# Output-weight loads moved from SyncE's DMA queue to ScalarE's in a hybrid Fourier/SSD mixer layer

## The chip, the cores and the metric

The kernel runs on one core of a Trainium2 chip. The metric is the device time of one execution in microseconds; the figure to compare is the median of several runs. TensorE (PE) does the matrix products, VectorE (DVE), ScalarE (ACT) and GpSimd (POOL) the elementwise work, and SyncE (SP) starts the DMA transfers. Loads of TensorE's stationary operand are listed as PEld.

## The reference

One layer of a generator over 2048 latent tokens with 256 context tokens, model width 1024. A modulated RMSNorm feeds one input projection, whose columns split into a Fourier group and an SSD (Mamba-2) group; both are gated, joined and sent through one output projection of 2048 by 1024.

```python
def token_mixer(h, rows, cols, w_in, ...):
    u, zf, zs, xbc, dt_raw = jnp.split(h @ w_in, PROJ_SPLITS, axis=-1)
    four = fourier_mixer(u, zf, w_fourier, b_fourier)
    xbc = depthwise_conv_grid(xbc, conv_w, conv_b, rows, cols)
    ssd, h_f, h_b = ssd_mixer(xbc, dt_raw, zs, ..., h0_f, h0_b)
    return jnp.concatenate([four, ssd], axis=-1), h_f, h_b

def fourier_mixer(u, zf, w_f, b_f):
    uf = u.astype(jnp.float32).reshape(bsz, length, N_FOURIER_GROUPS, FOURIER_GROUP)
    mixed = jnp.fft.fft2(uf, axes=(1, 3), norm='ortho').real.reshape(bsz, length, D_FOURIER)
    mixed = mixed.astype(u.dtype) @ w_f + b_f
    return mixed * jax.nn.silu(zf)

# in reference(), for the one layer:
    hx = rmsnorm(x, norm_w[i]) * (1.0 + scale[:, None]) + shift[:, None]
    x_mix, _, _ = token_mixer(hx, rows, GRID_W, *layer, h_f, h_b)
    x = x + gate[:, None] * (x_mix @ w_out[i])
    return rmsnorm(x, final_norm_w)
```

The products are computed with operands split into a high and a low part (float32r), so that one product of the reference is three matrix products in the kernel: high by high, high by low and low by high.

## The kernel before, in words

The kernel runs in stages that overlap at their ends.

1. Normalisation and transposition give the normalised input as two large tiles, `hh` (high) and `hl` (low), each 128 partitions by 8 by 2048. Then follow the input projections, the convolution and the preparation of the SSD scan. In the convolution stage the output weights are also scaled, split and stored to the DRAM scratch `wo_d` (16 blocks of 128 rows, high and low).
2. A backward scan writes its share of the SSD output to DRAM (`yb_d`).
3. The Fourier stage. `f_table` and `f_step2` prepare the tables `ab` and the intermediate `xf`, which lie in the room of `hh` and `hl` that is no longer needed. `f_mm(dt, h, i)` is half of a product for one of four channel tiles `dt` (in the order 0, 3, 1, 2) and one half `h` of the frequencies: 12 matrix products into one PSUM tile of tag `mm`, of which there are six. After the second half (i = 1) `f_gate` copies it to the tile `q32` on ScalarE (one buffer), VectorE makes the sum and the difference `yy` (two buffers), and GpSimd and VectorE multiply them into the gate table `zf`. `zf` holds the gate of one channel tile, 128 by 2048, has two buffers, and is loaded by `zf_load` from `zfT_d`; the finished product is stored from the same tile to `fm_d`. So the third and the fourth `zf` load wait for the stores of the first and the second tile. The eight products run in the order (0,0), (0,1), (3,0), (3,1), (1,0), (2,0), (1,1), (2,1), as (dt, h).
4. The units. The last stage handles 64 units, one per chunk c of 128 tokens and group g of 6 heads, in steps: `s1` loads decay rows (`rt`, `lt`), `cb` and `chl`, makes the arguments `parg` on TensorE, their exponential `w` on ScalarE and the product `w` times `cb` on VectorE; `s2` loads `yb`, `zs`, `xg` and `bt` and applies the carried state (`pyo`); `s3` advances the state (`pst`); `s4` makes the chunk's output (`py`) and its gate; `s5` normalises it (`pn`, `mh`, `ml`); `s6` does the output projection (`po`) with the weights `wos` and the Fourier part `fm`, which `fm_half` loads from `fm_d`. The loop body for u has s1 and s2 of unit u + 1, s3 and s4 of u, s5 of u - 1, s6 of u - 2.

The output weights come back from `wo_d` in four groups of four blocks, one group for each g; a block is two loads (high and low). `wplace` gives their places, all in the room of `hh` and `hl`:

```python
    wplace = [((hl, 1536), (hh, 1536)), ((hl, 0), (hl, 1024)), ((hl, 512), (hh, 1024)), ((hh, 0), (hh, 512))]
```

Group 0 takes the last quarter of both tiles, free when the last gate projection has read it. Group 1 takes room of `xf` for h = 0, group 2 that for h = 1, and group 3 that of the tables `ab`, which every Fourier product reads.

What sets the order: the instructions are written in Python, and a scheduler lays them out per engine by the order of writing and a model of when each becomes ready; each engine then executes its list in order and waits at an instruction whose inputs or room are not there. `tc.issue_after(ins)` around a block adds that its instructions come behind `ins` on the engine of `ins`. `interleave` mixes the list `side` of Fourier steps with the last projections; what is left of it is issued just before the units. Before the change every DMA is begun by SyncE through `load` (line 63), the weight loads too. Group 0 is issued behind the interleaved part, group 1 as a step of `side` ahead of the last two Fourier products, groups 2 and 3 in the unit loop at u = 0 and 1, behind the last `fm_d` store (`fo["st"]`) and the `bt` load of the next unit. The helper `copy` (line 68) is a ScalarE activation; line 72 is the low part of a split.

Of the kernel before, what the change touches and what calls it, by code (L numbers as in the profile page):

```python
# [9 lines left out]
F32 = mybir.dt.float32  # L10
# [29 lines left out]
def rev(ap):  # L40
    dims = [list(d) for d in ap.ap]
    off = ap.offset
    for d in dims[1:]:
        off += d[0] * (d[1] - 1)
        d[0] = -d[0]
    return bass.AP(ap.tensor, off, dims)
# [3 lines left out]
def mixer_layer(ctx: ExitStack, tc: tile.TileContext, A: dict, out: bass.AP, taps=None):  # L50
    nc = tc.nc
    mm = nc.tensor.matmul

    def pool(name, bufs=1, space=None, stack=ctx, side=None):
        kw = {"space": space} if space is not None else {}
        if side is not None:
            kw["side"] = side
        if space != DRAM:
            kw["reuse_waits"] = "tile"
        return stack.enter_context(tc.tile_pool(name=name, bufs=bufs, **kw))  # L60

    def load(dst, src):
        return nc.sync.dma_start(out=dst, in_=src).ins
# [3 lines left out]
    def copy(dst, src):  # L67
        return nc.scalar.activation(dst, src, AF.Copy).ins  # L68
# [8 lines left out]
    def scratch(name, shape, dtype=F32):  # L77
        return dram.tile(list(shape), dtype, name=name)
# [14 lines left out]
    wo_d = scratch("wo_d", [16, P, 2, D], F32R)  # L93
# [46 lines left out]
    p1 = ctx.enter_context(ExitStack())  # L140
# [70 lines left out]
    with ExitStack() as p0, tc.issue_after(pre):  # L211
# [130 lines left out]
        for op in 'n1 n2 m1 n3 m2 m3'.split():  # L342
            if op == "n1":
                norm_finish(xn1, hh, hl, 512, 0)
            elif op[0] == "n":
                b = int(op[1])
# [3 lines left out]
            else:  # L350
                b = int(op[1])
# [4 lines left out]
    with ExitStack() as pu:  # L356
# [144 lines left out]
        for n2 in range(16):  # L501
# [3 lines left out]
            for k in range(KT):  # L505
                a = hh[:, k].rearrange("p (a b) -> p b a", b=16)[:, n2]
                b = hl[:, k].rearrange("p (a b) -> p b a", b=16)[:, n2]
# [3 lines left out]
            with tc.issue_after(mu):  # L511
                if n2 in dt_work:
                    fn, i = dt_work[n2]
# [257 lines left out]
    with ExitStack() as psc:  # L771
        sp = pool("sp3", 2, stack=psc)
        st = {}
# [60 lines left out]
        side = []  # L834
# [3 lines left out]
        for n, a in enumerate(seq):  # L838
            if n + AHEAD < len(seq):
                side.append((0.0, scan_prep(*seq[n + AHEAD])))  # L840
            dr, c, g = a
# [7 lines left out]
    wos = {}  # L849
# [3 lines left out]
    def w_load(n):  # L853
        r, k = 2 * (n % 4), worder[n]
        wos[k] = tuple(t[:, r:r + 2, c:c + 512] for t, c in wplace[n // 4])
        for i in range(2):
            load(wos[k][i].bitcast(F32), wo_d[k, :, i].rearrange("p (a b) -> p a b", a=2).bitcast(F32))

    def w_group(g):
        for n in range(4 * g, 4 * g + 4):  # L860
            w_load(n)
# [10 lines left out]
    fo = {"new": main_psum}  # L872
# [23 lines left out]
    def zf_load(dt):  # L896
        def go():
            zf = zft[dt] = fb.tile([P, 16, P], F32, name="zf", tag="zf")
            load(zf[:].rearrange("p a b -> p (a b)"), zfT_d[dt])
            if dt != 2:  # L900
                nc.scalar.activation(zf, zf, AF.Silu)
            nc.gpsimd.tensor_tensor(out=zf[:, :, 64], in0=zf[:, :, 64], in1=ye[:, dt], op=ALU.mult)
        return go

    def f_table(j):
        def go():
            for i in range(2):
                pa = main_psum()
                mm(pa, c64[i], wfs[j], start=True, stop=True)
                copy(ab(i, 0, j), pa)  # L910
                nc.vector.tensor_tensor(out=ab(i, 1, j), in0=pa, in1=ab(i, 0, j).bitcast(F32), op=ALU.subtract)
            if j < 3:
                g_load(0, j + 1)
        return go
# [30 lines left out]
    def f_gate(dt, p0, p1, parts):  # L945
        zf = zft[dt]
        q32 = fb.tile([P, 512], F32, name="q32", tag="q32", bufs=1)
        copy(q32, p1)
        for sign in range(2):
            yy = fb.tile([P, 512], F32, name="yy", tag="yy")  # L950
            nc.vector.scalar_tensor_tensor(out=yy, in0=p0, scalar=bf[:, dt:dt + 1], in1=q32,
                                           op0=ALU.add, op1=ALU.add if sign == 0 else ALU.subtract)
            for yv, k1, nt in parts[sign](yy):
                a = k1 if sign == 0 else P - k1 - nt * yv.shape[-1] + 1
                zv = zf[:, :, a:a + nt * yv.shape[-1]]
                if sign == 1:
                    zv = rev(zv)
                if nt > 1:
                    zv = zv.rearrange("p a (t b) -> p t a b", t=nt)
                (nc.vector if sign else nc.gpsimd).tensor_tensor(out=zv, in0=yv, in1=zv, op=ALU.mult)  # L960

    def f_mm(dt, h, i):
        def go():
            po = fo[i] = fo["new"]()
            f_half(po, dt, i, lambda *a: xf(*a, h))
            if i == 0:
                return

            def cut(yy):
                return yy[:].rearrange("p (t a b) -> p t a b", t=8, b=4)  # L970

            def minus(yy):
                if h:
                    return [(cut(yy), 32, 8)]
                return [(cut(yy)[:, 0, :, 1:4], 1, 1), (cut(yy)[:, 1:], 4, 7)]

            f_gate(dt, fo[0], fo[1], (lambda yy: [(cut(yy), 32 * h, 8)], minus))
            if h == 1:
                fo["st"] = store(fm_d[:, :, dt, :].rearrange("c p w -> p c w"), zft[dt])
        return go  # L980
# [28 lines left out]
    side = [(1.7, f_table(j)) for j in range(4)]  # L1009
# [8 lines left out]
    for n, (dt, h) in enumerate(fmm):  # L1018
        if n in (4, 5):
            side.append((0.0, zf_load(dt)))  # L1020
        if n == 6:
            side.append((0.0, lambda: w_group(1)))
        side += [(2.6, f_mm(dt, h, i)) for i in range(2)]
    left = interleave(zs_ops([(i, (3,)) for i in range(19, 7, -1)]), side, 10, .75)
    wa1 = P2["wa1"]
# [16 lines left out]
    w_group(0)  # L1042
    for _, fn in left:
        fn()
    p1.close()
    ps = pool("ps2", space=PSUM)
    fo["new"] = lambda: ps.tile([P, 512], F32, name="pft", tag="out", bufs=2)
    pre2 = preload(LNEXP)
    units = {}

    def s1(u):
        c, g = divmod(u, G)
        d = units[u] = {}
        if g == 0:
            sml = wa1.tile([P, 3, H], F32, name="sml4", tag="sml")
            load(sml, smf_d[:, c])
        else:
            sml = units[u - 1]["sml"]
        d["sml"] = sml
        r, l = rt[u % 2], lt[u % 2]  # L1060
        cs = slice(c * P, c * P + P)
        for dr in range(2):
            hsl = slice(dr * H + g * HG, dr * H + (g + 1) * HG)
            load(r[32 * dr + 12:32 * dr + 14, :].rearrange("o (h w) -> o h w", w=P).bitcast(F32),
                 cum_d[:, hsl, cs].bitcast(F32))
            for s in range(2):
                load(l[32 * dr + 6 * s:32 * dr + 6 * s + 6, dr].bitcast(F32), q_d[s, hsl, cs].bitcast(F32))
        cb = wa1.tile([P, P], F32, name="cb", tag="cb")
        load(cb, cb_d[c, :, g])
        chl = wa1.tile([P, 2, P], F32R, name="chl", tag="chl")  # L1070
        load(chl[:].bitcast(F32), chl_d[c, :, g].bitcast(F32))
        d["chl"] = chl
        w = wa1.tile([P, HG, P], F32, name="w", tag="w")
        for h2 in range(2):
            cols = slice(384 * h2, 384 * h2 + 384)
            pa = []
            for dr in range(2):
                po = ps.tile([P, 3, P], F32, name="parg", tag="arg", bufs=2)
                mm(po, l[:, dr], r[:, cols], start=True, stop=True)  # L1079
                pa.append(po)  # L1080
            nc.vector.copy_predicated(out=pa[0], mask=msk[:].unsqueeze(1).broadcast_to([P, 3, P]), data=pa[1])  # L1081
            with tc.issue_after(pre2):
                d["exp"] = nc.scalar.activation(w[:, 3 * h2:3 * h2 + 3], pa[0], AF.Exp).ins  # L1083
        nc.vector.tensor_tensor(out=w, in0=w, in1=cb[:].unsqueeze(1).broadcast_to([P, HG, P]), op=ALU.mult)  # L1084
        d["w"] = w
# [162 lines left out]
    for u in range(NU + 2):  # L1248
        if u + 1 < NU:
            if u > 0:  # L1250
                s1(u + 1)
            s2(u + 1)
        if u < 2:
            with tc.issue_after(fo["st"]), tc.issue_after(units[u + 1]["ld"]):
                w_group(u + 2)
        if u < NU:
            s3(u)
            s4(u)
        if 1 <= u <= NU:
            s5(u - 1)  # L1260
        if u >= 2:
            s6(u - 2)
# [110 lines left out]
```

## Time and profile before

| what | value |
|---|---|
| median of 3 runs | 1908.56 us (1906.04 to 1908.92) |
| profiled execution: its own time | 1912.61 us |
| profiled execution: span | 1910.8 us |
| TensorE busy | 1809.4 us, 95% |
| VectorE, ScalarE, GpSimd busy | 66%, 46%, 47% |
| mean granted TensorE clock | 0.977 |
| DMA | 301.80 MB, 158 GB/s over the span |

The profile is one execution recorded by the hardware. Times are in microseconds from the start of the span unless marked ns. In a row of the timeline stand the start, the length, the engine, the line of the kernel, the operation, output <- inputs by the program's names, and in square brackets the idle time just before it with what ended it. SPq is SyncE's queue of DMA issues: the length there is that of the issue, not of the transfer. The chain is the work that ended last, followed back from the last instruction; a DMA in it stands with its time from issue to landing. The stage of the change lies between about 1190 and 1340 us.

### The profile page before, as it was taken

What the parts mean: (1) busy time and instruction counts of PE and PEld (TensorE: products, weight loads), DVE (VectorE), ACT (ScalarE), POOL (GpSimd) and SP (SyncE); (2) the same over time, 40 slices, a digit from 0 to 9 for tenths busy, and PEclk for the clock granted to TensorE, in tenths of its full rate; (3) what the DMA queues carried; (4) which work ended last, traced back from release to release, by engine and by line L of the source; (5) the groups of instructions that cost most, each with busy time, mean ns of one, the idle gap of its engine ahead of it and who ended that gap; (6) DMA issues with size and microseconds to landing.
All of it is one profiled execution on the core that took longest, in us unless ns stands there. A gap on an engine that the chain in (4) does not pass through costs nothing.

```text
span 1910.8 us, 28132 instructions
## 1 busy us (share of the span) xinstructions
PE 1809.4 (95%) x9142; PEld 1492.4 (78%) x9142; DVE 1258.5 (66%) x1809; ACT 873.9 (46%) x1968; POOL 906.2 (47%) x791
## 2 busy tenths in 40 slices
PE   6989999999999999989999999957999999999997
PEld 2779988888888888878888877845778777777776
DVE  3744569788888897557665622334677777667865
ACT  3632235445445455346666653223444444435443
POOL 1320034224123134178787732145777777668742
PEclk8999999999999999999999999977999999999999
DMA  7432344535445345367776774786445444444441
GB/s 256 166 93 77 90 131 151 171 113 166 138 130 160 122 129 174 120 200 217 213 218 206 216 247 136 224 287 218 125 143 151 130 132 134 147 124 138 144 137 44
DMA packets 291332, 301.80 MB, mean 158 GB/s; under 512 B 34098, under 2 KB 242066, under 8 KB 290675
## 3 DMA queue, kind: packets, MB, share of 16 engines
q1 hardware_dynamic: 291186, 300.01, 50.6%
q8 instruction: 73, 1.20, 0.3%
q14 instruction: 73, 0.59, 0.1%
HBM read 196.82 MB, written 103.10 MB: 157 GB/s over the span
## 4 chain that ended last, share of the span: by engine, by line
PE 75%; DMA 9%; DVE 5%; POOL 5%; issue 3%; ACT 2%; SPq 1%; POOLq 0%; DVEq 0%; ACTq 0%
PE pj L178 11%; PE pj L177 11%; PE pj L176 11%; PE po L1212 6%; PE po L1210 6%; PE po L1211 6%; PE py L1151 2%; PE parg L1079 2%; POOL sl L72 2%; PE pj L508 1%; PE pj L509 1%; PE pj L510 1%; PE py L1154 1%; DMA ev<-in_wout 1%; PE ptr L569 1%
## 5 line engine op out<-in xcount | busy, mean ns | idle before, releaser
L178 PE MATMUL pj<-hh,wl 128*128 128x512 f32 x1152 | 452.6, 393 | 0.8 <-POOL wl L72 0.8
L177 PE MATMUL pj<-hl,wh 128*128 128x512 f32 x1152 | 452.1, 392 | 0.0
L176 PE MATMUL pj<-hh,wh 128*128 128x512 f32 x1152 | 450.0, 394 | 2.1 <-ACT img L68 1.6
L636 DVE SCALAR_TENSOR_TENSOR pacc<-img,c_convw,pacc 128x1024 f32<-128x1024 f32 x320 | 410.0, 1287 | 58.5 <-ACT pacc L633 49.2
L72 POOL TENSOR_TENSOR wl<-raw,wh 128x1024 fp32r<-128x1024 f32 x48 | 116.5, 2428 | 345.4 <-ACT wh L68 294.8
L178 PEld LDWEIGHTS pj<-hh,wl 128*128 128x128 f32 x1152 | 216.4, 188 | 47.4 <-POOL wl L72 1.4
L176 PEld LDWEIGHTS pj<-hh,wh 128*128 128x128 f32 x1152 | 217.0, 188 | 44.4 <-ACT img L68 2.3
L177 PEld LDWEIGHTS pj<-hl,wh 128*128 128x128 f32 x1152 | 216.6, 188 | 40.9 <-issue 1.8
L807 ACT ACTIVATE xd<-xt,smb 128x64 f32<-128x64 f32 x384 | 100.8, 336 | 80.2 <-POOL yb L811 78.5
L1210 PE MATMUL po<-hl,mh 128*128 128x512 f32 x288 | 117.5, 408 | 0.7 <-ACT mh L68 0.4
L1211 PE MATMUL po<-hh,mh 128*128 128x512 f32 x288 | 114.8, 399 | 0.0
L1081 DVE COPY_PREDICATED parg<-msk,parg 128x384 f32<-128x384 uint8 x128 | 71.1, 556 | 64.1 <-PE parg L1079 63.7
L1212 PE MATMUL po<-hl,ml 128*128 128x512 f32 x288 | 109.8, 401 | 2.6 <-POOL ml L72 2.4
L1083 ACT ACTIVATE w<-parg 128x384 f32<-128x384 f32 x128 | 62.3, 486 | 104.8 <-DVE parg L1081 104.5
L72 DVE TENSOR_TENSOR xl<-xw,xh 128x384 fp32r<-128x384 f32 x76 | 63.7, 843 | 59.3 <-ACT xh L68 57.9
L1120 POOL TENSOR_TENSOR ts<-ts,yb 128x384 f32<-128x384 f32 x64 | 73.6, 1150 | 57.6 <-issue 27.2
L1079 PE MATMUL parg<-rt,lt 128*128 128x384 f32 x256 | 88.0, 372 | 11.2 <-DMA rt<-cum_d 4.1
L72 POOL TENSOR_TENSOR ml<-gt,mh 128x384 fp32r<-128x384 f32 x64 | 68.4, 1068 | 58.8 <-ACT mh L68 55.4
L68 ACT ACTIVATE xh<-xw 128x384 fp32r<-128x384 f32 x136 | 69.9, 516 | 55.2 <-PE pst L1138 14.9
L1084 DVE TENSOR_TENSOR w<-w,cb 128x768 f32<-128x768 f32 x64 | 81.6, 1275 | 12.1 <-ACT w L1083 10.9
L72 DVE TENSOR_TENSOR sl<-hbk,sh 128x384 fp32r<-128x384 f32 x64 | 59.9, 937 | 38.4 <-ACT sh L68 38.2
L72 POOL TENSOR_TENSOR sl<-ev,sh 128x512 fp32r<-128x512 f32 x32 | 42.1, 1317 | 89.1 <-DMA wo_d<-sl 38.3
(388 smaller groups left out, 4132.7 us busy)
## 6 DMA issues: line engine op xcount, KB each, us to landing
raw<-in_win SPq DMA_DIRECT2D x48, 512.0 KB
xt<-xtok_d SPq DMA_DIRECT2D x80, 192.0 KB
xtok_d<-tk SPq DMA_DIRECT2D x48, 256.0 KB
zsT_d<-ev SPq DMA_DIRECT2D x48, 256.0 KB
yb_d<-yb SPq DMA_DIRECT2D x64, 192.0 KB
yb<-yb_d SPq DMA_DIRECT2D x64, 192.0 KB
zs<-zsT_d SPq DMA_DIRECT2D x64, 192.0 KB
xg<-xtok_d SPq DMA_DIRECT2D x64, 192.0 KB
```

What stands on the lines that cost most here:

```text
L72: (lo_engine or nc.vector).tensor_tensor(out=lo, in0=src, in1=hi.bitcast(F32), op=ALU.subtract)
L176: mm(po, wh[:, k], a, start=(k == 0), stop=False)
L177: mm(po, wh[:, k], b, start=False, stop=False)
L178: done["mm"] = mm(po, wl[:, k], a, start=False, stop=(k == KT - 1)).ins
L636: nc.vector.scalar_tensor_tensor(out=acc, in0=im[:, r0 + dy:r0 + dy + 16, dx:dx + GRID_W], scalar=tap(t), in1=acc, op0=ALU.mult, op1=ALU.add)
L807: nc.scalar.activation(xd[:, h], d["x"][:, h], AF.Copy, scale=smb[:, 3, c, g * HG + h:g * HG + h + 1])
L1079: mm(po, l[:, dr], r[:, cols], start=True, stop=True)
L1084: nc.vector.tensor_tensor(out=w, in0=w, in1=cb[:].unsqueeze(1).broadcast_to([P, HG, P]), op=ALU.mult)
L1120: nc.gpsimd.tensor_tensor(out=ts, in0=ts, in1=yb, op=ALU.add)
L1210: mm(po, a, wh[:, i], start=(g == 0 and q == 0), stop=False)
L1211: mm(po, a, wl[:, i], start=False, stop=False)
L1212: mm(po, b, wh[:, i], start=False, stop=(g == 3 and q == 3))
```

## The change

The 32 weight loads are begun by ScalarE instead of SyncE. The Fourier gate remembers its copy to `q32`, the ScalarE instruction that follows the last read of the group's room, in `fo["q"]`; groups 1, 2 and 3 are issued behind it. Group 1 keeps its place in `side`. Groups 2 and 3 are issued together after the last Fourier product, ahead of the units, and no longer in the unit loop; the conditions on `fo["st"]` and on the `bt` load are gone.

```diff
         for i in range(2):
-            load(wos[k][i].bitcast(F32), wo_d[k, :, i].rearrange("p (a b) -> p a b", a=2).bitcast(F32))
+            nc.scalar.dma_start(out=wos[k][i].bitcast(F32),
+                                in_=wo_d[k, :, i].rearrange("p (a b) -> p a b", a=2).bitcast(F32))
+
+    def w_after(g):
+        with tc.issue_after(fo["q"]):
+            w_group(g)
 ...
     def f_gate(dt, p0, p1, parts):
         zf = zft[dt]
         q32 = fb.tile([P, 512], F32, name="q32", tag="q32", bufs=1)
-        copy(q32, p1)
+        fo["q"] = copy(q32, p1)
 ...
         if n == 6:
-            side.append((0.0, lambda: w_group(1)))
+            side.append((0.0, lambda: w_after(1)))
 ...
     w_group(0)
     for _, fn in left:
         fn()
+    for g in (2, 3):
+        w_after(g)
     p1.close()
 ...
             s2(u + 1)
-        if u < 2:
-            with tc.issue_after(fo["st"]), tc.issue_after(units[u + 1]["ld"]):
-                w_group(u + 2)
         if u < NU:
             s3(u)
             s4(u)
```

## The prediction

> **What bounds the kernel now.** I read the page first, then busy time by stretches around the change, then the chain of work that ended last inside them, then the single queues.
>
> ```profile
> span 1910.8 us, 28132 instructions
> PE 1809.4 (95%) x9142; PEld 1492.4 (78%) x9142; DVE 1258.5 (66%) x1809; ACT 873.9 (46%) x1968; POOL 906.2 (47%) x791
> PE 75%; DMA 9%; DVE 5%; POOL 5%; issue 3%; ACT 2%; SPq 1%; POOLq 0%; DVEq 0%; ACTq 0%
> ```
>
> Over the whole span TensorE is the bound: 1809.4 of 1910.8 us busy, so some 101 us of idle time are all that any change of order can win. The 9% of DMA in the chain are where the change works. The stretches (columns: window, length, busy us and instructions of PE, PEld, DVE, ACT, POOL, granted clock, DMA share, GB/s):
>
> ```profile
> 1190.00:1250.90 60.90, 60.85 (x289) 50.84 (x287) 21.73 (x35) 18.87 (x32) 17.94 (x15) 1.00 0.71 225
> 1250.90:1267.30 16.40, 0.00 (x0) 0.01 (x1) 4.67 (x8) 0.60 (x1) 3.82 (x4) 0.58 0.61 232
> 1267.30:1285.00 17.70, 13.88 (x57) 10.56 (x58) 10.84 (x17) 5.75 (x13) 9.50 (x10) 0.62 1.03 328
> 1285.00:1313.50 28.50, 13.96 (x53) 10.47 (x52) 8.94 (x17) 7.36 (x17) 7.91 (x8) 0.64 0.76 257
> 1313.50:1340.00 26.50, 25.51 (x137) 20.80 (x136) 14.62 (x25) 8.99 (x21) 21.19 (x22) 1.00 0.59 171
> ```
>
> TensorE is full to 1250.9, wholly idle for 16.4 us, then idle for 3.8 and 14.5 us of the next two stretches, and full again from 1313.5. So 34.7 us of the 101 lie between the last Fourier product and the steady state of the units; a shift of the point 1313.5 passes on to the end one for one, since TensorE is 96% busy just behind it. The chain through the hole (start, length, what):
>
> ```profile
> 1249.31 12.74 DMA zf<-zfT_d
> ...
> 1265.79 1.40 DVE yy L951 x2
> ...
> 1267.32 0.66 PE pyo L1115
> ...
> 1273.36 7.32 DMA hl<-wo_d
> 1280.70 8.38 DMA c_fnw<-in_fnw
> ...
> 1291.47 9.62 DMA hh<-wo_d
> 1301.12 4.57 DMA rt<-cum_d
> ...
> 1308.78 3.79 DMA chl<-chl_d
> ```
>
> Two things end last there: the gate table zf of the last Fourier tile (dt 2), landing at 1262.05, and transfers that stand behind output-weight loads. The queue of SyncE shows why:
>
> ```profile
> 1239.65 0.37 SPq L63 DMA_DIRECT2D fm_d<-zf  x1
> 1240.97 8.29 SPq L63 DMA_DIRECT2D hl<-wo_d  x8
> 1249.31 1.23 SPq L63 DMA_DIRECT2D zf<-zfT_d  x1
> 1266.04 2.84 SPq L63 DMA_DIRECT2D fm_d<-zf  x2
> 1268.98 2.94 SPq L63 DMA_DIRECT2D hl<-wo_d  x1
> ```
>
> The zf load stands behind all eight loads of group 1. Also, the chain's hl load issued at 1273.36 lands at 1280.68, and the fnw load, eighth in the queue's order after it, is issued at 1280.70; the hh load of 1291.47 lands at 1301.09 and the rt load, again the eighth after it, goes at 1301.12. So a transfer here starts only when the one eight places earlier has landed: at most eight are under way.
>
> **The change part by part.** Sizes, and the price of one issue (ns least/median/most):
>
> ```profile
> hl<-wo_d SPq DMA_DIRECT2D x16, 512.0 KB
> fm_d<-zf SPq DMA_DIRECT2D x4, 1024.0 KB
> zf<-zfT_d SPq DMA_DIRECT2D x2, 1024.0 KB
> L63 SPq DMA_DIRECT2D hl<-wo_d x16: 360/480/3402, 1216.4 to 1275.7; - x16
> ```
>
> *The issue of 32 loads* (16 hl, 16 hh) leaves SyncE and goes to ScalarE: 32 x 0.48 = 15 us of ScalarE's own time, against 46% busy, in place of the same on SyncE. The 3.4 us maximum stands right behind an fm_d store, as does the 2.94 us one. ScalarE could be held like that or, its queue being another, not at all: 0 to 3.4 us for a load next to a store.
>
> *Groups 0 and 1 on ScalarE.* Before 1250.9 I cost them at nothing: ScalarE is busy 18.87 of 60.9 us there, TensorE has six output buffers, and every delayed q copy of line 68 is hidden by the zf wait, as the next rows show: the last q copy sat idle 19.23 us. If zf landed at once, a held copy would cost up to the 3.4 us above.
>
> ```profile
> 1264.98 0.60 ACT L68 ACTIVATE q<-pj 128x512 f32<-128x512 f32 x1 [19.23 <-DVE yy L951]
> 1268.94 0.49 ACT L1083 ACTIVATE w<-parg 128x384 f32<-128x384 f32 x1 [3.37 <-DVE parg L1081]
> 1271.48 0.47 ACT L1083 ACTIVATE w<-parg 128x384 f32<-128x384 f32 x1
> ```
>
> *The zf load.* It no longer shares SyncE's queue with group 1. Whether the limit of eight is kept per queue or for both together, the trace of before, in which SyncE issues everything, can't say. Under a common limit its issue stays at 1249.31; with limits apart it goes earlier. Its 12.74 us have as bounds 1 MB at the full rate of the rows below, 1.05 MB / 389 GB/s = 2.7 us, and 12.74 unchanged. I take twice the full-rate time, 5.4 us, as two queues that share evenly: landing at 1254.7, 7.3 us earlier, and pyo then at 1254.7 + 5.3 (the 1262.05 to 1267.32 of the chain) = 1260.0. The earliest possible is about 1253.0: TensorE's last product at 1250.9, q copy 0.6, two yy 1.4.
>
> The Trainium skill ("DMA: Bandwidth & Descriptors", Queues, rings and completion order) says that each DMA engine takes turns between the queues it has work for, a packet at a time. That speaks for sharing rather than for strict order; that two queues were ever loaded at once, no run here shows.
>
> *Groups 2 and 3* are no longer behind the fm_d store and a unit's bt load; all sixteen come right after the last q copy. This is the added wait: behind them on ScalarE stand the exponentials of units 0 and 1 (line 1083), and for those wait VectorE's products w and TensorE's py, pn and po. How long? The DMA engines have no room:
>
> ```profile
> 1250.00:1255.00 5.00, 0.85 (x5) 0.46 (x3) 0.00 (x0) 0.00 (x0) 0.00 (x0) 0.85 1.04 389
> 1265.00:1270.00 5.00, 2.68 (x8) 2.61 (x9) 4.71 (x7) 1.63 (x4) 1.65 (x3) 0.50 0.61 172
> 1270.00:1275.00 5.00, 3.02 (x18) 1.97 (x17) 3.45 (x5) 1.65 (x4) 5.00 (x5) 0.84 1.01 252
> 1280.00:1285.00 5.00, 4.60 (x17) 3.28 (x14) 2.04 (x5) 1.04 (x2) 1.00 (x1) 0.58 1.05 390
> ```
>
> At 389 to 390 GB/s one 0.524 MB load takes 1.34 us. Whichever comes first, zf and group 1 together keep the engines to about 1262 as now. From there eight of the sixteen must land before the last can be issued: 8 x 1.34 = 10.8, so ScalarE is free at about 1273, 4 us later than its 1268.94 of now. Bounds: not held at all (its loads issued freely), and held some 14 us more (last rival).
>
> The first exponential is then 4 us late, but both arguments are ready by then: now 1268.94 to py at 1273.73 are 4.8 us; then two exponentials, 0.49 + 0.47, and the product, 1.69, make 2.7. So py starts at 1275.7, 2.0 us later than now:
>
> ```profile
> 1271.99 1.69 DVE L1084 TENSOR_TENSOR w<-w,cb 128x768 f32<-128x768 f32 x1 [0.44 <-ACT w L1083]
> 1273.73 1.36 PE L1151 MATMUL py<-w,xg 128*64 128x128 f32 x12 [1.28 <-DVE w L1084]
> 1289.52 0.66 PE L1079 MATMUL parg<-rt,lt 128*128 128x384 f32 x2 [2.08 <-DMA lt<-q_d]
> 1290.87 0.56 PE L1115 MATMUL pyo<-sh,chl 128*128 128x384 f32 x1 [0.69 <-DMA chl<-chl_d]
> 1305.82 1.01 PE L1079 MATMUL parg<-rt,lt 128*128 128x384 f32 x2 [4.09 <-DMA rt<-cum_d]
> 1308.69 0.69 PE L1115 MATMUL pyo<-sh,chl 128*128 128x384 f32 x1 [1.85 <-DMA chl<-chl_d]
> 1312.70 0.42 PE L1115 MATMUL pyo<-sh,chl 128*128 128x384 f32 x1 [1.08 <-DMA chl<-chl_d]
> ```
>
> *What SyncE's transfers do then.* Sixteen loads from 1262 end at 1262 + 21.5 = 1283.5; the two fm_d stores, 2.1 MB, and fnw, 0.5 MB, are 6.9 us more at that rate: 1290.4. So the first chl of these rows comes about when it does now, 1290.8, and its two waits, 2.08 + 0.69 = 2.8, swallow the 2.0 us and give nothing. The next three waits, 4.09 + 1.85 + 1.08 = 7.0 us, are on transfers that stand behind the eight hh loads issued from 1289.98 on, which are over by then: they go. Late next is the units' own chain of ScalarE, VectorE and GpSimd.
>
> **Sum:** +2.0 - 2.0 - 7.0 = -7.0 us. The earlier zf adds nothing of its own, because ScalarE is held past it. Against the profiled execution (1912.61 us, span 1910.8) that is 1905.6; that execution lies 4.05 above the median 1908.56, so in terms of the median 1901.5, rounded to 1901. The likeliest case's own range is 1896 to 1905: 5 us either way for the half-rate guess and for the two waits.
>
> **The rivals.**
>
> *More is won: ScalarE is not held.* If the loads are issued without waiting for landings, or the exponentials get in between, pyo starts 7.3 us earlier and all five waits go, 9.8 us: 17.1, so 1891.5. The most is 14.3 (pyo at 1253.0) + 9.8 = 24.1: 1884.5. For it: ScalarE's work is light here, and its own queue starts empty. Against it: the eight-back rule holds at both places quoted.
>
> *Nothing is won: the transfers end when they did.* The bytes are the same and the DMA engines are full from 1267 to 1285 (share 1.03). If the order of landings stays, the median stays at 1908.6. Against it: the share is 0.61 and 0.76 in the stretches on either side, so the engines do lose time that order can give back.
>
> The Trainium skill ("DMA: Bandwidth & Descriptors", Issuing engines are not separate DMA queues) states that issuing from several engines saves only the sequencer's issue time. By that the result would be this rival; I give it little, as the waits above are on queue order and not on rate.
>
> *Slower: ScalarE held too long.* The place is ScalarE between the last q copy and its first exponential. If the fm_d stores and the next unit's loads are counted between the sixteen, their time comes on top: the stores took most of 1265 to 1275 (172 and 252 GB/s, 10 us), fnw and some 0.9 MB of a unit's loads 3.7 more, so ScalarE is free at 1273 + 13.7 = 1286.7. py is then 15.7 late, 9.8 of it returned by the waits: +5.9, 1914.5. It decides at a first exponential after 1280.8 (2.0 + 7.8 = 9.8). For it: a store already holds the next issue 2.94 us. Against: SyncE's stores wait for the gate and come after the q copy.
>
> **How the numbers follow.** Likeliest (-7.0) 0.45; more won 0.25; nothing won 0.13; slower 0.17. About 0.2%, 3.8 us, is what a measurement of this kernel can tell from no change: faster 0.70, same 0.13, slower 0.17. The range, 1887 to 1915, takes in the likeliest, the unchanged and most of the slower case, and leaves out the outer part of "more won".
>
> **What would show it.** zf landing near 1254 and pyo near 1260 confirm the sharing; zf still near 1262 refutes it. ScalarE's first exponential of line 1083 near 1273 confirms the hold: before 1266 is the second case, after 1281 the last. Waits of parg and pyo on rt and chl under 1 us before the first fm product, which would start near 1306 in place of 1313.3, confirm the gain. The prediction is wrong if the program's order of loads and exponentials on ScalarE is another than assumed, or if a changed order lengthens the units behind 1340.

## The result and the profile after

The change made the kernel slower: 1920.22 us median (1919.29 to 1925.72) against 1908.73 for the kernel before (1906.04 to 1908.92), a ratio of 1.007 (95% interval 1.0049 to 1.009). The prediction, 1901 us in a range of 1887 to 1915, missed in size and in direction. The profiled execution of the changed kernel took 1920.63 us against 1912.61, 8.0 more.

The page of the changed kernel: span, busy time by engine, shares of the chain of work that ended last.

```profile
span 1918.8 us, 28127 instructions
PE 1804.8 (94%) x9142; PEld 1488.9 (78%) x9142; DVE 1258.2 (66%) x1809; ACT 872.6 (45%) x1968; POOL 903.5 (47%) x791
PE 75%; DMA 10%; POOL 5%; DVE 4%; issue 3%; ACT 2%; SPq 1%; ACTq 0%; POOLq 0%; DVEq 0%
```

TensorE is busy 4.6 us less and the span is 8.0 us longer: the loss is idle time of TensorE, 114.0 us in place of 101.4. Where does it lie? First the five stretches around the change, with the columns of the prediction's table:

```profile
1190.00:1250.90 60.90, 59.58 (x284) 49.80 (x282) 21.18 (x34) 16.17 (x27) 12.60 (x9) 1.00 0.72 235
1250.90:1267.30 16.40, 3.54 (x10) 3.02 (x10) 7.60 (x12) 2.43 (x5) 11.39 (x12) 0.58 0.78 274
1267.30:1285.00 17.70, 0.00 (x0) 0.00 (x0) 0.27 (x1) 0.00 (x0) 0.23 (x1) 0.58 1.06 349
1285.00:1313.50 28.50, 19.12 (x89) 14.73 (x90) 12.43 (x23) 10.18 (x24) 17.67 (x18) 0.78 0.70 240
1313.50:1340.00 26.50, 23.91 (x150) 19.23 (x149) 17.82 (x33) 12.94 (x31) 21.18 (x21) 1.00 0.42 127
```

The hole has a new form. TensorE runs ten products in the second stretch, where it ran none, and then none at all for 17.7 us, where it ran 57. VectorE, ScalarE and GpSimd all but stand still there too (0.27, 0.00 and 0.23 us busy), while the DMA share is 1.06. TensorE's timeline has the ends of that hole (start, length, line, operation, idle time before it and what ended it):

```profile
1263.43 0.66 PE L1122 MATMUL pyo<-sh,chl 128*128 128x384 f32 x1 [13.85 <-DVE yy L956]
...
1289.45 0.69 PE L1086 MATMUL parg<-rt,lt 128*128 128x384 f32 x1 [22.48 <-ACT w L1090]
...
1292.72 1.55 PE L1158 MATMUL py<-w,xg 128*64 128x128 f32 x12 [0.71 <-DVE w L1091]
...
1309.88 0.50 PE L1217 MATMUL po<-hl,fm 128*128 128x512 f32 x1
```

The first pyo comes at 1263.43 instead of 1267.32, as the change promises (1.3 us of it lie ahead of the stage: the last Fourier product begins at 1248.85 instead of 1250.12), but the first py comes at 1292.72 instead of 1273.73. What ends the 22.48 us is ScalarE's first exponential `w` (line 1090, 1083 before), and ScalarE was held by its own loads (ACTq is its queue of issues):

```profile
1261.08 0.60 ACT L68 ACTIVATE q<-pj 128x512 f32<-128x512 f32 x1 [8.18 <-DVE yy L956]
1261.11 0.37 ACTq L857 DMA_DIRECT2D hl<-wo_d  x1
...
1265.58 0.37 ACTq L857 DMA_DIRECT2D hl<-wo_d  x1
1276.86 12.01 ACTq L857 DMA_DIRECT2D hh<-wo_d  x9
1288.91 0.49 ACT L1090 ACTIVATE w<-parg 128x384 f32<-128x384 f32 x1 [27.23 <-DMA hh<-wo_d]
```

Seven loads go between 1261.11 and 1265.58, the eighth at 1276.86, the last just before 1288.91. The chain of work that ended last tells what the eighth waited for (start, length, what; a DMA from issue to landing):

```profile
1239.65 10.93 DMA fm_d<-zf
1250.60 7.56 DMA zf<-zfT_d
...
1262.15 14.68 DMA fm_d<-zf
1276.86 0.40 ACTq L857
```

A store to `fm_d`, begun by SyncE at 1262.15, lands 14.68 us later at 1276.83, and ScalarE's load goes 0.03 us after that. The trace keeps with each transfer the semaphore by which it reports its landing. The program has eight of them, given out in turn over both queues (1734 transfers, 216 or 217 to each), and a transfer goes only when the last one on its semaphore has landed. The load of 1276.86 has the semaphore of that store.

That hold looks like the whole explanation, and it is not. From 1190 to 1340 TensorE executed 536 instructions before (289 + 0 + 57 + 53 + 137) and 533 after (284 + 10 + 0 + 89 + 150). The long stretches on both sides say the same. The kernel before:

```profile
0.00:1325.00 1325.00, 1250.31 (x6057) 1045.28 (x6058) 841.80 (x1038) 614.16 (x1306) 511.90 (x420) 0.97 0.54 170
1325.00:1890.00 565.00, 546.86 (x3034) 437.50 (x3033) 410.90 (x759) 255.62 (x651) 390.55 (x369) 0.99 0.44 133
1890.00:1919.00 29.00, 12.28 (x54) 9.62 (x52) 5.82 (x13) 4.09 (x11) 3.80 (x4) 0.87 0.07 26
```

The changed kernel:

```profile
0.00:1325.00 1325.00, 1244.80 (x6059) 1042.44 (x6060) 840.73 (x1037) 613.55 (x1307) 512.91 (x421) 0.97 0.54 171
1325.00:1890.00 565.00, 539.68 (x3004) 430.49 (x3004) 409.50 (x755) 252.99 (x646) 385.00 (x366) 1.00 0.43 133
1890.00:1919.00 29.00, 20.29 (x85) 15.99 (x81) 7.93 (x18) 6.01 (x16) 5.54 (x5) 0.85 0.07 26
```

At 1325 the changed kernel has 6059 TensorE instructions behind it, the kernel before 6057: the hold has been repaid but for 1 or 2 us, by work of later units that TensorE did with less waiting. (Its count is 2 ahead, but it came to the stage 1.3 us early; by TensorE's busy time still to come, 560.0 us against 559.1, it is 0.8 us behind.) In the next 565 us, in which nothing was edited, it executes 30 fewer and is idle for 25.3 us instead of 18.1. It is there that it falls behind. A count of instructions doesn't weigh them by length, so this says where to look rather than how many microseconds. The largest of TensorE's waits between 1325 and 1890 (waiting line, what it waited for: us in all, times, longest), first before:

```profile
PE pst L1136 <- DVE ts L1119: 5.6, 9, 1.5
PE po L1212 <- POOL ml L72: 2.4, 2, 1.7
```

and after:

```profile
PE parg L1086 <- DVE parg L1088: 4.9, 4, 1.9
PE po L1219 <- POOL ml L72: 4.4, 5, 1.7
PE pst L1143 <- DVE ts L1126: 3.7, 7, 1.0
```

No transfer is among them, and no single wait in this stretch is over 3 us: they are many small ones on other engines, at other places than before. The order of instructions on each engine is drawn by the scheduler that builds the program, and this edit drew it anew for what follows. From turn u = 4 of the unit loop on, 2385 of the 2670 instructions of TensorE stand at another place in its order than before. So there were two theories. *Stage:* the held ScalarE costs the time. *Order:* the new order of the units costs it.

### The profile page after: what moved, and what is told of

It reads as the page before. It is cut to its first block, busy times and chain, and to the rows that moved or that the text cites. A ratio compares the mean times of both kernels' runs of the same rounds, so it can differ in the third digit from the quotient of the medians.

```text
span 1918.8 us, 28127 instructions
## 1 busy us (share of the span) xinstructions
PE 1804.8 (94%) x9142; PEld 1488.9 (78%) x9142; DVE 1258.2 (66%) x1809; ACT 872.6 (45%) x1968; POOL 903.5 (47%) x791
## 4 chain that ended last, share of the span: by engine, by line
PE 75%; DMA 10%; POOL 5%; DVE 4%; issue 3%; ACT 2%; SPq 1%; ACTq 0%; POOLq 0%; DVEq 0%
PE pj L177 12%; PE pj L178 12%; PE pj L176 12%; PE po L1219 6%; PE po L1217 6%; PE po L1218 6%; PE py L1158 2%; POOL sl L72 2%; PE parg L1086 2%; DMA fm_d<-zf 1%; PE pj L508 1%; PE pj L509 1%; PE pj L510 1%; PE py L1161 1%; PE ptr L569 1%
## 5 line engine op out<-in xcount | busy, mean ns | idle before, releaser
L1218 PE MATMUL po<-hh,mh 128*128 128x512 f32 x288 | 114.0, 396 | 0.0
L72 POOL TENSOR_TENSOR sl<-hf,sh 128x384 fp32r<-128x384 f32 x64 | 73.2, 1145 | 49.0 <-ACT sh L68 46.7
```

Of the source, the lines that this page charges most:

```text
L72: (lo_engine or nc.vector).tensor_tensor(out=lo, in0=src, in1=hi.bitcast(F32), op=ALU.subtract)
L1218: mm(po, a, wl[:, i], start=False, stop=False)
```

## The experiments

Most kernels below hold the order of the units fixed. From turn u = 4 on, each engine's instructions, SyncE's transfers among them, are chained in a list recorded from another kernel. The links order instructions of one engine and ask for no semaphore. The kernel before with its own list was not run; that the links as such cost little is seen below in a kernel that has them, in before's order, and takes 1.0001. "Before's order" and "after's order" name the lists.

```diff
+        if u == 4:
+            mark = nc.cur_bb.bb.instructions[-1]
 ...
+    keep_order(tc, mark)   # for each engine, in the listed order:
+                           #   tc.add_manual_dep(ins, prev.name, <order only, no semaphore>)
```

Ratios are to the kernel before, on the same chip, with 95% intervals; they are worked out from all runs and can differ by 0.1% from the ratio of the two medians.

### Stage and order apart

The kernel before with after's order of the units:

> The kernel before, unchanged up to the unit loop's turn u = 4; from there on each engine issues the units' instructions in the order of the changed kernel. Order theory (the hold of ScalarE is repaid by about 1320 us, and the 8 us of the profile are made in the units by another issuing order): slower than before, ratio 1.003 to 1.007, median 1914 to 1922. Hold theory (ScalarE held until 1288.9 passes on to the end): no hold here, so as before, 1906 to 1911, ratio within 0.2%.

The changed kernel with before's order:

> The changed kernel with all its weight loads on ScalarE, but from u = 4 on each engine issues the units' instructions in the order of the kernel before. Order theory: back to before or a little under, 1904 to 1911, ratio 0.998 to 1.002, with ScalarE's first exponential still near 1289. Hold theory: as slow as the changed kernel, 1917 to 1922, ratio 1.005 to 1.007.

The first took 1923.51 us against 1912.08, 1.006 (1.0044 to 1.0076); the second 1918.18, 1.0029 (1.0016 to 1.0041). With the change itself they make a table of four:

| | before's order of units | after's order of units |
|---|---|---|
| stage of before | 1 | 1.006 |
| stage of the change | 1.0029 | 1.007 |

The order alone costs 0.6% with no weight load moved; the stage costs 0.29% in before's order. The 0.1% between the two kernels in after's order is within their intervals. The long stretches agree. The kernel before with after's order:

```profile
0.00:1325.00 1325.00, 1251.93 (x6060) 1046.28 (x6060) 844.16 (x1042) 616.25 (x1309) 514.17 (x421) 0.97 0.54 171
1325.00:1890.00 565.00, 539.82 (x2994) 431.02 (x2996) 408.22 (x750) 251.76 (x642) 384.07 (x366) 1.00 0.44 132
```

and the changed kernel with before's order:

```profile
0.00:1325.00 1325.00, 1241.94 (x6033) 1038.62 (x6034) 836.75 (x1030) 610.26 (x1298) 506.83 (x416) 0.97 0.54 170
1325.00:1890.00 565.00, 547.01 (x3045) 437.38 (x3044) 413.77 (x764) 258.18 (x657) 391.77 (x373) 0.99 0.44 133
```

After's order gives 2994 instructions and 539.82 us of TensorE's time behind 1325, like the change; before's gives 3045 and 547.01, like before. In before's order the stage's loss shows in part where it arises: 24 instructions fewer than before at 1325. At the later rate of 565 us for 3034 instructions, 0.186 us each, that is some 4.5 us by this estimate; 1.75 us of them were late before the stage began (its last Fourier product begins at 1251.86 against 1250.12), so some 2.7 us arise in it, half of the 5.5 us of the ratio 1.0029. Both theories hold in part; the order is the larger.

### Where in the units the order costs

After's order for turns 46 and later only, on the kernel before:

> The kernel before; turns 4 to 45 of the unit loop in its own order, and turns from 46 on in the order of the changed kernel. In the run with the whole order of the changed kernel the lag behind before was +6.5 us at 1500, -2.1 at 1700 and +7.7 at 1900. Late theory (what is lost early is won back, and only the last twenty turns cost): ratio 1.003 to 1.007. Spread theory (every part of the order costs in proportion): 1.001 to 1.003.

and for turns 4 to 45 only:

> The kernel before; turns 4 to 45 in the order of the changed kernel, from 46 on in its own. Late theory: ratio 0.998 to 1.002. Spread theory: 1.003 to 1.005.

The late half took 1924.58 us, 1.0075 (1.0061 to 1.0088); the early half 1918.91, 1.0046 (1.003 to 1.0062). Each costs, and together (1.006) they cost no more than the late one alone, so the parts don't add up, and no single half carries the cost. Neither theory put on record had both numbers: the late one allowed 1.002 at most for the early half, the spread one 1.003 for the late half. A list cut in two has a seam that neither whole list has, and what a seam costs was not measured. Why before's order suits the units better stays open. Taking over the order of one engine alone was not tried, since the orders of the engines depend on one another.

### What holds ScalarE

The change with the last two `fm_d` stores put behind the sixteen loads in the order of all DMAs, before's order:

```diff
             if h == 1:
-                fo["st"] = store(fm_d[:, :, dt, :].rearrange("c p w -> p c w"), zft[dt])
+                def put():
+                    return store(fm_d[:, :, dt, :].rearrange("c p w -> p c w"), zft[dt])
+                if dt in dts[:2]:
+                    put()
+                else:
+                    fo.setdefault("put", []).append(put)
 ...
+    for put in fo["put"]:          # loads: the last weight load
+        tc.add_manual_dep(put(), loads.name, <order only>)
```

> The changed kernel with the last two fm_d stores placed behind the sixteen loads in the order of all DMAs, and the units from u = 4 on in the order of the kernel before. If ScalarE was held because its loads wait for SyncE's stores eight places ahead (one limit of eight for both queues), the first exponential comes at 1273 to 1278 in place of 1288.9, as eight of the loads must land after 1262 at 1.34 us each. If the limits are apart and ScalarE waits only for its own loads and a full data path, it stays at 1285 to 1290. Time: order theory 1900 to 1910; hold theory 1905 to 1912, some 10 us under the run with the order alone put back.

It took 1915.23 us, 1.0019 (1.0006 to 1.0032), and ScalarE's timeline is

```profile
1263.02 0.60 ACT L135 ACTIVATE q<-pj 128x512 f32<-128x512 f32 x1 [6.95 <-DVE yy L1023]
1266.79 18.22 ACTq L924 DMA_DIRECT2D hh<-wo_d  x9
1285.05 0.49 ACT L1166 ACTIVATE w<-parg 128x384 f32<-128x384 f32 x1 [21.44 <-DMA hh<-wo_d]
```

against this in the change with before's order:

```profile
1280.38 13.08 ACTq L924 DMA_DIRECT2D hh<-wo_d  x9
1293.50 0.49 ACT L1157 ACTIVATE w<-parg 128x384 f32<-128x384 f32 x1 [28.24 <-DMA hh<-wo_d]
```

With no store among them the eighth load goes at 1266.79, not 1280.38. The first exponential, at 1285.05, lies where it was expected if the two queues had limits apart, so its time alone doesn't decide. The semaphores do: in the change with before's order the load of 1280.38 has the semaphore of the store of 1265.73 and goes when that has landed. So a load on ScalarE's queue does wait for a transfer of SyncE's, and the eight are one limit for both queues together. The hold shrinks by 28.24 - 21.44 = 6.8 us, and no more, because the remaining nine loads now take 18.22 us to issue. Here SyncE's loads for the units (chl, lt, yb, bt) stand among them in the turn of the semaphores: seven of SyncE's to sixteen of ScalarE's. From 1270.98 on ScalarE's loads take four of the eight semaphores and SyncE's the other four, so that four are left to ScalarE, and the load that its last one waits for, eight places ahead in the turn, is the twelfth of the sixteen and not the eighth. The DMA share is 0.97 meanwhile (1263 to 1285), so part of the hold is plain transfer time; how much of it the semaphores add was not measured. SyncE's queue in that kernel:

```profile
1268.49 4.20 SPq L130 DMA_DIRECT2D chl<-chl_d  x2
...
1283.04 5.71 SPq L130 DMA_DIRECT2D fm_d<-zf  x2
```

The loads for the units go from 1268.49 on, in the midst of the hold, and the stores only near its end. So the stores make a quarter of the hold (6.8 of 28.24). The gain in time against the change in before's order, 0.1%, is inside the intervals, and 1915 us is longer than either theory had it (1912 at most).

### Parts of the change

Groups 0 and 1 on ScalarE, groups 2 and 3 on SyncE at their old places, before's order:

```diff
-            nc.scalar.dma_start(out=wos[k][i].bitcast(F32),
+            (nc.scalar if n < 8 else nc.sync).dma_start(out=wos[k][i].bitcast(F32),
 ...
-    for g in (2, 3):
-        w_after(g)
 ...
+        if u < 2:
+            with tc.issue_after(fo["st"]), tc.issue_after(units[u + 1]["ld"]):
+                w_group(u + 2)
```

> Groups 0 and 1 by ScalarE, groups 2 and 3 by SyncE at their old places; units from u = 4 on in the order of the kernel before. Tells the price of the second half of the change. Order theory: ScalarE's first exponential near 1265, 4 us earlier than before, since the last zf load lands near 1258; time 1903 to 1908. Hold theory: without the sixteen loads the hold is gone, also 1903 to 1908, and so well under the run with the order alone put back (1917 to 1922); the order theory has the two within 5 us.

1911.78 us, 1.0001 (0.999 to 1.0011): nothing, where both theories had expected 1903 to 1908. Its chain has

```profile
1243.03 12.58 DMA fm_d<-zf
1255.61 0.02 issue
1255.63 7.35 DMA hl<-wo_d
```

and its first exponential comes at 1269.78 (1268.94 before), although the last Fourier product began 3.0 us later (1253.13 against 1250.12). Group 1 gets out of zf's way on SyncE and back into its way on the DMA engines: the store that must land before zf can be loaded takes 12.58 us there. So the early part of the change, with some 2 us won inside the stage, nets to nothing that the time shows, and the 0.29% come with groups 2 and 3.

The change with groups 2 and 3 issued by ScalarE behind the exponentials of units 1 and 2, before's order:

```diff
-    for g in (2, 3):
-        w_after(g)
 ...
+        if u < 2:
+            with tc.issue_after(units[u + 1]["exp"]):
+                w_group(u + 2)
```

> The changed kernel (all loads on ScalarE, group 1 ahead of the last zf load) with groups 2 and 3 behind the exponentials of units 1 and 2 instead of behind the last q copy; units from turn 4 on in the order of before. The hold ahead of the first exponential goes: it comes near 1265 to 1270 in place of 1289 to 1293. Hold theory of what is left (ratio 1.0029 with the order put back): ratio 0.997 to 1.001. If the hold only moves behind the exponentials, onto the sq and mh copies: 1.001 to 1.004.

1917.06 us, 1.0023 (1.0008 to 1.0039), no better than 1.0029 by more than the intervals. ScalarE's timeline:

```profile
1272.07 0.49 ACT L1155 ACTIVATE w<-parg 128x384 f32<-128x384 f32 x1 [3.39 <-DVE parg L1153]
...
1294.28 0.49 ACT L1155 ACTIVATE w<-parg 128x384 f32<-128x384 f32 x1 [9.45 <-DMA hh<-wo_d]
...
1299.40 12.12 ACTq L924 DMA_DIRECT2D hh<-wo_d  x7
```

The first exponential is free. The hold comes later, in parts: 9.45 us ahead of an exponential at 1294.28, and seven more loads that take 12.12 us to issue.

### Better places, and who issues

On the kernel before, all on SyncE, group 1 queued behind the last zf load, before's order:

```diff
-            load(zf..., zfT_d[dt])
+            fo["zl"] = load(zf..., zfT_d[dt])
 ...
+    def w_first():                  # group 1 right behind the last zf load
+        with tc.issue_after(fo["zl"]):
+            w_group(1)
 ...
-            side.append((0.0, lambda: w_group(1)))
+            side.append((0.0, w_first))
```

> The kernel before with all loads on SyncE, and group 1 queued behind the last zf load instead of ahead of it; units from turn 4 on in the order of before. If the 16 us hole is the zf load's place in the queue, zf lands near 1252 in place of 1262 (issue behind the fm_d store's landing at 1247.4, then 1 MB at 389 GB/s and a latency), pyo starts near 1257 in place of 1267.3, and 3 to 8 us of the 10 reach the end: ratio 0.996 to 0.9985. If the bytes alone decide (the data path is full to 1262 whatever comes first), zf comes early but what follows does not: ratio 0.999 to 1.001.

1906.82 us against 1912.47, 0.9974 (0.9964 to 0.9984): faster. Its chain:

```profile
1241.58 7.73 DMA fm_d<-zf
1249.32 4.86 DMA zf<-zfT_d
```

The store lands in 7.73 us and zf in 4.86, not 12.74: this is what the change was after, with nothing moved to ScalarE. Then groups 2 and 3 one turn later as well:

```diff
-        if u < 2:
-            with tc.issue_after(fo["st"]), tc.issue_after(units[u + 1]["ld"]):
-                w_group(u + 2)
+        if 1 <= u < 3:
+            with tc.issue_after(units[u + 1]["ld"]):
+                w_group(u + 1)
```

> As the run with group 1 behind zf, and groups 2 and 3 one turn later, behind the loads of units 2 and 3, still on SyncE. If the units wait for transfers that stand behind the weight loads (9.8 us of waits on lt, rt and chl between 1287 and 1313 in before), most of those waits go: ratio 0.991 to 0.996. If they wait for a full data path, no more than the run with group 1 alone: within 0.1% of it.

1903.67 us, 0.9959 (0.9946 to 0.9972), ahead of both kernels; what groups 2 and 3 add to the step before is not outside the intervals. The same edits with the order of the units left to the scheduler:

> The same edits as the run with groups 2 and 3 later (0.9959), but the units' order left to the scheduler. Order theory (any new order of the units costs, by chance, from nothing to 0.7%): slower than that run, ratio 0.996 to 1.003. If the order of the changed kernel was bad because of its late weight loads and not by chance, this kernel, whose loads delay nothing, keeps the whole gain: 0.994 to 0.997.

1911.73 us against 1912.07, 0.9998 (0.9985 to 1.0011). The 0.4% that the placing wins are lost to the newly drawn order, the same effect as in the change. Last, the same places in the scheduler's order of all transfers, and the same order of the units, with ScalarE as the issuer:

```diff
-            load(wos[k][i].bitcast(F32), ...)
+            nc.scalar.dma_start(out=wos[k][i].bitcast(F32), ...)
+            # ordered behind fo["zl"] (group 1) or units[n // 4]["ld"] (groups 2, 3)
```

> As the run with groups 2 and 3 later, at the same places in the order of all DMAs (behind the last zf load and behind the loads of units 2 and 3), but begun by ScalarE; units from turn 4 on in the order of before. If the place of the loads decides and not the queue that begins them: within 0.15% of 0.9959. If a queue that also computes pays for every wait of its loads: slower than that run by 0.2% or more, with gaps of ScalarE ahead of its exponentials that end at loads.

1910.32 us against 1912.07, 0.9991 (0.9976 to 1.0007). So 0.3% are lost against SyncE as issuer. But the places are equal in the scheduler's order alone: nothing makes ScalarE wait for SyncE to have issued the zf load. With SyncE as issuer zf goes first:

```profile
1247.43 0.32 SPq L130 DMA_DIRECT2D zf<-zfT_d  x1
1247.85 6.10 SPq L130 DMA_DIRECT2D hl<-wo_d  x8
```

With ScalarE as issuer group 1 goes from 1243.85 on, ahead of zf, which is issued at 1248.78 and takes 8.39 us to land instead of 4.95. The first pyo comes 11.5 us after the start of the last Fourier product instead of 6.5. ScalarE's timeline shows this, and computing instructions that were held by loads:

```profile
1243.85 13.72 ACTq L924 DMA_DIRECT2D hl<-wo_d  x8
1257.69 0.60 ACT L135 ACTIVATE q<-pj 128x512 f32<-128x512 f32 x1 [13.32 <-DMA hl<-wo_d]
...
1281.79 0.52 ACT L1235 ACTIVATE sq<-gt 128x384 f32<-128x384 f32 x1 [9.59 <-DMA hl<-wo_d]
```

How much of the 0.3% is the lost place and how much the held engine, this run can't tell; with a wait that keeps group 1 behind zf it was not run. The Trainium skill ("DMA: Bandwidth & Descriptors", Issuing engines are not separate DMA queues) says that issuing from several engines saves only the sequencer's time to start the transfers. The comparison agrees that the second queue gains nothing.

## Why the prediction was wrong

*The zf load.* Predicted: issue at 1249.31, 5.4 us at half rate, landing 1254.7, pyo at 1260.0. Measured: issue 1250.60, 7.56 us, landing 1258.16, pyo 1263.43. Sharing was right and mis-sized by 2.2 us. The issue is late for a reason the prediction left out: zf waits for the first `fm_d` store to land, and that store now shares too, 10.93 us against 7.73 where SyncE has it without group 1 beside it. The gain was 3.9 us and not 7.3, and 1.3 of it lay ahead of the stage. The Trainium skill ("DMA: Bandwidth & Descriptors", Queues, rings and completion order), cited there for sharing by turns, agrees in kind: zf became faster and the stores slower.

*ScalarE held.* This is the first step that failed. The term "eight of the sixteen must land before the last can be issued", 8 x 1.34 = 10.8, was to free ScalarE at 1273; the first exponential came at 1288.91. The term counted only ScalarE's own loads and only at the full rate. Under the common limit, which the prediction left open, nine transfers of SyncE stand among the sixteen loads in the turn of the semaphores: two stores and seven loads for the units. So the last load, issued at 1288.50, waits for the eleventh of the sixteen to land and not for the eighth, and the eighth itself waits for a store. The stores make 6.8 us of the hold. The rival "Slower: ScalarE held too long" had it at 1286.7, by the right mechanism. The argument against it was that the stores "come after the q copy": they do, but only by 1 us, so that the first, at 1262.15, is issued among the loads.

*The waits behind it.* py was to be 2.0 late and was 19.0 late. But the first product with `fm`, named as the sign of the gain at "near 1306", came at 1309.88 against 1313.3, and by 1325 TensorE had done as much as before. So the 7.0 us of waits were swallowed by the hold, and the sign appeared while the time grew: a product that comes early says little when the scheduler may put it elsewhere among the others.

*What stands behind 1340.* This is the larger failure. The sum passed the shift of 1313.5 "to the end one for one". "If a changed order lengthens the units behind 1340" is named as what would make it wrong, and it has no term, no price and no case among the rivals. It costs 0.6% alone, some 11 us, more than any term of the sum. The slower rival, which has no such term either, gave 1914.5; the change in before's order comes to 1.0029 x 1908.56 = 1914.1. That the two agree is luck, since the rival had py 15.7 late and the waits behind it returning 9.8.

*The sum.* -7.0 was predicted, +11.5 measured between the medians (0.7% by the ratio). By the table of four, 0.29% of it is the stage in before's order, and 0.41% comes on top with the order. Taken the other way round, the order is 0.6% and the stage 0.1%; the two ways agree within the intervals.

## What to carry to other kernels

Before loads are given to an engine that computes, look for what its in-order queue will hold behind them, and find out which transfers share completion semaphores: here those of both queues did, slow stores included. A scheduler that draws the order anew can cost as much far from an edit as the edit itself wins or loses, so compare an edit in a fixed order before judging it. Here the gain lay in the place of a load within one queue: the group put behind the load that TensorE waits for was worth 0.26%. On a second queue that place was not kept, and most of the 0.41% won by then was gone.

## What the runs showed of the hardware

Three things that I had not expected. As this program is built, at most eight transfers are under way over both queues, because it gives out eight completion semaphores in turn: ScalarE's load went at 1276.86, 0.03 us after the landing of SyncE's store, which had the same semaphore. Whether the chip would allow more, these runs don't tell. With two queues loaded, the 1 MB store to `fm_d` took 10.93 to 14.68 us against 7.73, while the 1 MB load of zf in that company took 7.56 against 12.74 in one queue behind group 1. And a hold of 27 us on one engine, with TensorE wholly idle for 17.7 us of it, left TensorE's count of instructions 36 us later where it was in the kernel before.
